# GpSimd's weight subtractions in pieces of 256 columns in a two-block transformer kernel on Trainium2

## The chip, the core and the metric

The kernel runs on one core of one Trainium2 chip. The core has TensorE (PE in the profile) for matrix products, VectorE (DVE), ScalarE (ACT) and GpSimd (POOL) for elementwise work, and SyncE (SP), whose queue issues the DMAs here. Each engine works through its own list of instructions in order and waits on semaphores for the others. The metric is the device time of one execution in microseconds; less is better.

## The reference

The reference runs two transformer blocks of two layers each on a sequence of 512 tokens of width 1024, in float32. The first block mixes a sparse attention and a stick-breaking attention; the second uses a latent attention (MLA) in its first layer and a gated linear attention (GLA) in its second. Each layer ends in an MLP with a squared ReLU:

```
hn = rms_norm(x, norm_g[0])
...                                   # projections of hn @ w_in, attentions, output products
x = x + rms_norm(mixed, norm_g[1])
hf = rms_norm(x, norm_g[2])
ff = jnp.square(jax.nn.relu(hf @ w_ff1)) @ w_ff2
return x + rms_norm(ff, norm_g[3])
```

## The kernel before

Products are made to float32 accuracy from three passes of rounded operands. Each operand x is kept as a high part h, which is x rounded to the matmul's format (written by ScalarE), and a low part l = x − h. A product is then h·h + l·h + h·l, three matmuls that add up in one PSUM bank (`mac3`, L211 to L213; for products with tokens on the partitions L238 to L240).

Weights come in units. `wload` (L169) takes a unit of, as a rule, 8 k-tiles by 256 columns or 4 k-tiles by 512, and splits it in two halves by k-tile. For each half it issues one DMA into a raw buffer (`wraw`, three buffers), has ScalarE write the high part (`wh`, L190), and has GpSimd subtract it from the raw values to give the low part (`wl`, L194). Most halves hold 1024 values per partition, so that one GpSimd instruction works on 128x1024 values. With `both`, used near the start of a stage, the half is split once more between VectorE and GpSimd, and GpSimd's share is 128x512. The pool of weights has two buffers per name, and a raw buffer is free for the next DMA when both parts have been read from it.

VectorE makes the low parts of activations (L166, `split`), adds partial sums of the MLP's second product into y (L541, one input in PSUM), squares the MLP's hidden values (L529, with both inputs in SBUF), and applies residuals and normalisation: `residual` (L301) runs L308 and L309 in turn for eight k-tiles, `newton` (L283) three short instructions on the inverse root. In the first block's second product of the conditioning vectors, spread through the MLP, VectorE also runs L1380, which has one input in SBUF and one in PSUM. In the sparse attention, `nsa_cmp` runs L996 to L1006 on the compressed scores, and TensorE transposes the result in L1010. Within the layers, GpSimd also scales softmax values (L1047, L1764) and adds some sums of squares (L299, into `acc`).

The order of each engine's instructions comes from the order in which the program emits them and a scheduler that sorts them by need; DMAs of weights, of the conditioning matrix (`araw`) and of intermediate values all go through SP's queue. Generators interleave the stages: `tick` and `fill` put steps of a normalisation or of a background product between the matmuls of a running one.

Of the kernel before, what the change touches and what calls it, by code (L numbers as in the profile page):

```python
# [11 lines left out]
F32 = mybir.dt.float32  # L12
# [3 lines left out]
ALU = mybir.AluOpType  # L16
# [34 lines left out]
class Builder:  # L51
# [117 lines left out]
    def wload(self, ap, both=False, pool=None, raws=(), after=()):  # L169

        nc = self.nc
        aps = ap if isinstance(ap, list) else [ap]
        kt, n = aps[0].shape[1], sum(a.shape[2] for a in aps)
        h = self.t(pool or self.wp, [P, kt, n], F32R, tag="wh")
        l = self.t(pool or self.wp, [P, kt, n], F32R, tag="wl")
        hk = (kt + 1) // 2
        for a, b in ((0, hk), (hk, kt)):
            if a < b:
                if raws:
                    raw = raws[a > 0]  # L180
                else:
                    raw = self.t(self.wp, [P, b - a, n], F32, tag="wraw", bufs=3)
                    c = 0
                    for x in aps:
                        nc.sync.dma_start(raw[:, :, c:c + x.shape[2]], x[:, a:b])
                        c += x.shape[2]
                step = max(1, (b - a) // 2) if both else b - a
                for x in range(a, b, step):
                    z = min(b, x + step)
                    i = nc.scalar.copy(h[:, x:z], raw[:, x - a:z - a]).ins  # L190
                    for j in after:
                        self.tc.add_manual_dep(i, j.name, NOSYNC, reason="order")
                    e = nc.vector if both and x == a else nc.gpsimd
                    e.tensor_tensor(l[:, x:z], raw[:, x - a:z - a], h[:, x:z].bitcast(F32), op=ALU.subtract)  # L194
        return h, l

    def wload_turned(self, ap, w):

        nc = self.nc
        raw = self.t(self.wp, [P, 8, 64], F32, tag="wraw", bufs=3)  # L200
        nc.sync.dma_start(raw, ap)
        x = raw.rearrange("p k (a b e) -> p k a b e", a=2, b=2)
        h, lo = (o.rearrange("p k (b a e) -> p k b a e", a=2, b=2) for o in w)
        for b in range(2):
            nc.scalar.copy(h[:, :, b], x[:, :, :, b])
            nc.gpsimd.tensor_tensor(lo[:, :, b], x[:, :, :, b], h[:, :, b].bitcast(F32), op=ALU.subtract)
# [2144 lines left out]
```

## Time and profile before

| | |
|---|---|
| median of 3 runs | 3435.24 us (3432.82 to 3436.9) |
| profiled execution | 3436.59 us, span 3434.8 us |
| TensorE busy | 3264.5 us, 95% |
| VectorE busy | 2136.6 us, 62% |
| ScalarE busy | 1511.9 us, 44% |
| GpSimd busy | 1172.7 us, 34% |
| granted clock of TensorE, mean | 0.982 |

Busy times are sums over instructions, from the start of each to its end. An instruction that has started and stands still counts as busy. Idle time of an engine that nobody waits for costs nothing. A granted clock of 1.00 in a stretch is 2.4 GHz throughout; less means that part of the stretch ran at 1.2 GHz.

### The profile page before, as it was taken

How to read it: one execution, taken by the hardware profiler on the slowest of the kernel's cores; microseconds unless marked ns; L12 is line 12 of the kernel's file. 1: busy time of each engine (PE TensorE's matmuls, PEld its weight loads, DVE VectorE, ACT ScalarE, POOL GpSimd, SP SyncE). 2: the span in 40 equal slices, each digit the busy share in tenths (PEclk: the TensorE clock that was granted, in tenths of full speed). 3: DMA queues.
4: the chain of work that ended last, by engine and by line, in shares of the span. 5: the costliest groups of instructions: out<-in, count | busy, mean ns of one | idle time of the engine just before them, and what ended most of it. 6: DMA issues, size and time to landing. Idle time of an engine off the chain costs nothing.

```text
span 3434.8 us, 48977 instructions
## 1 busy us (share of the span) xinstructions
PE 3264.5 (95%) x18723; PEld 2825.8 (82%) x18723; DVE 2136.6 (62%) x4036; ACT 1511.9 (44%) x3323; POOL 1172.7 (34%) x688
## 2 busy tenths in 40 slices
PE   8899989999889998999999999999999899989998
PEld 8788778778878877778888879888888888878887
DVE  6855676885875567676577765333344767873445
ACT  5445544232544555432256664422222566653223
POOL 3333334444323333434422222222232222124443
PEclk8999999999999999999999999999999999999999
DMA  5212464553321245465321131121222211123332
GB/s 177 65 62 71 143 195 127 189 183 110 108 68 59 71 141 178 143 201 178 93 69 33 48 98 60 62 62 62 62 62 64 67 64 55 61 78 100 98 96 70
DMA packets 262097, 337.68 MB, mean 98 GB/s; under 512 B 17107, under 2 KB 178110, under 8 KB 261734
## 3 DMA queue, kind: packets, MB, share of 16 engines
q1 hardware_dynamic: 261862, 334.55, 31.0%
q8 instruction: 147, 2.41, 0.3%
q14 instruction: 88, 0.72, 0.1%
HBM read 305.98 MB, written 28.52 MB: 97 GB/s over the span
## 4 chain that ended last, share of the span: by engine, by line
PE 68%; DVE 17%; ACT 6%; issue 5%; DMA 3%; POOL 1%; SPq 0%; DVEq 0%; ACTq 0%; POOLq 0%
PE mm L211 15%; PE mm L213 15%; PE mm L212 15%; PE s L211 4%; PE s L212 4%; PE s L213 4%; PE s L280 2%; DMA araw<-in_ada_w_dram 2%; ACT wh L190 1%; DVE tp L1380 1%; PE tp L1065 1%; POOL wl L194 1%; DVE y L308 1%; PE mm L238 1%; PE mm L239 1%
## 5 line engine op out<-in xcount | busy, mean ns | idle before, releaser
L194 POOL TENSOR_TENSOR wl<-wraw,wh 128x1024 fp32r<-128x1024 f32 (+2 forms) x424 | 990.7, 2355 | 1748.3 <-ACT wh L190 1698.6
L211 PE MATMUL mm<-h,wh 128*128 128x512 f32 (+1 forms) x1916 | 722.6, 378 | 28.2 <-ACT h L332 8.8
L212 PE MATMUL mm<-h,wl 128*128 128x512 f32 (+1 forms) x1916 | 712.0, 372 | 0.5 <-DVE wl L194 0.4
L213 PE MATMUL mm<-h,wh 128*128 128x512 f32 (+1 forms) x1916 | 709.4, 371 | 2.1 <-DVE h L333 1.8
L190 ACT CAST wh<-wraw 128x1024 fp32r<-128x1024 f32 (+3 forms) x454 | 429.0, 967 | 493.8 <-issue 290.6
L211 PEld LDWEIGHTS mm<-h,wh 128*128 128x128 f32 x1916 | 367.6, 192 | 89.4 <-ACT h L332 9.6
L213 PEld LDWEIGHTS mm<-h,wh 128*128 128x128 f32 x1916 | 367.0, 192 | 64.0 <-DVE h L333 3.1
L212 PEld LDWEIGHTS mm<-h,wl 128*128 128x128 f32 x1916 | 368.1, 192 | 52.2 <-DVE wl L194 0.8
L529 DVE TENSOR_TENSOR t<-t 128x512 f32<-128x512 f32 (+1 forms) x140 | 173.0, 1235 | 253.1 <-ACT hid L525 252.9
L211 PE MATMUL mm<-hid,wh 128*128 128x512 f32 (+1 forms) x848 | 293.8, 346 | 11.8 <-DVE y L541 9.6
L212 PE MATMUL mm<-hid,wl 128*128 128x512 f32 (+1 forms) x848 | 290.9, 343 | 0.0
L213 PE MATMUL mm<-hid,wh 128*128 128x512 f32 (+1 forms) x848 | 290.5, 343 | 0.0
L1380 DVE SCALAR_TENSOR_TENSOR tp<-araw,sc,tp 128x512 f32<-128x512 f32 x280 | 200.5, 749 | 51.1 <-DMA araw<-in_ada_w_dram 50.0
L541 DVE TENSOR_TENSOR y<-y,mm 128x512 f32<-128x512 f32 (+1 forms) x192 | 105.4, 549 | 193.7 <-PE mm L213 193.5
L530 DVE TENSOR_TENSOR hid<-t,hid 128x512 fp32r<-128x512 f32 (+1 forms) x176 | 205.6, 1172 | 31.5 <-ACT t L527 26.3
L213 PE MATMUL s<-hid,wh 128*128 128x512 f32 (+1 forms) x560 | 208.7, 373 | 0.0
L211 PE MATMUL s<-hid,wh 128*128 128x512 f32 (+1 forms) x560 | 208.6, 373 | 0.0
L212 PE MATMUL s<-hid,wl 128*128 128x512 f32 (+1 forms) x560 | 208.2, 372 | 0.0
L525 ACT ACTIVATE hid<-t 128x512 fp32r<-128x512 f32 (+1 forms) x176 | 97.1, 554 | 241.7 <-DVE t L522 165.9
L211 PEld LDWEIGHTS mm<-hid,wh 128*128 128x128 f32 x848 | 160.0, 189 | 38.2 <-DVE y L541 6.8
L212 PEld LDWEIGHTS mm<-hid,wl 128*128 128x128 f32 x848 | 160.1, 189 | 20.9
L213 PEld LDWEIGHTS mm<-hid,wh 128*128 128x128 f32 x848 | 160.0, 189 | 21.0
(686 smaller groups left out, 7337.1 us busy)
## 6 DMA issues: line engine op xcount, KB each, us to landing
wraw<-in_w_ff_dram SPq DMA_DIRECT2D x128, 512.0 KB
wraw<-in_mlp_w_dram SPq DMA_DIRECT2D x128, 512.0 KB
araw<-in_ada_w_dram SPq DMA_DIRECT2D x96, 512.0 KB
wraw<-in_w_in_dram SPq DMA_DIRECT2D x68, 512.0 KB
raw<-in_cmp_w_dram SPq DMA_DIRECT2D x16, 512.0 KB
td<-t SPq DMA_DIRECT2D x32, 256.0 KB
h<-td SPq DMA_DIRECT2D x32, 256.0 KB
wraw<-in_w_out_dram SPq DMA_DIRECT2D x16, 512.0 KB
```

The source lines that it names most:

```text
L190: i = nc.scalar.copy(h[:, x:z], raw[:, x - a:z - a]).ins
L194: e.tensor_tensor(l[:, x:z], raw[:, x - a:z - a], h[:, x:z].bitcast(F32), op=ALU.subtract)
L211: nc.tensor.matmul(ps, wh, mh, start=first, stop=False)
L212: nc.tensor.matmul(ps, wl, mh, start=False, stop=False)
L213: nc.tensor.matmul(ps, wh, ml, start=False, stop=last)
L238: nc.tensor.matmul(ps, h[:, sl], w[0][:, k, :n], start=k == 0, stop=False)
L280: self.nc.tensor.matmul(ps, self.ones, acc, start=first, stop=last)
L525: nc.scalar.activation(h, a, AF.Square)
L529: nc.vector.tensor_tensor(a, a, a, op=ALU.mult)
L530: nc.vector.tensor_tensor(lo, a, h.bitcast(F32), op=ALU.subtract)
L541: nc.vector.tensor_tensor(y, y, ps, op=ALU.add)
L1380: nc.vector.scalar_tensor_tensor(a, raw[:, k], sc, a, op0=ALU.mult, op1=ALU.add)
```

## The change

GpSimd's subtraction is written as a loop over the k-tiles of the half and, in each, over runs of at most 256 columns. VectorE's share under `both` stays one instruction.

```diff
-                    e = nc.vector if both and x == a else nc.gpsimd
-                    e.tensor_tensor(l[:, x:z], raw[:, x - a:z - a], h[:, x:z].bitcast(F32), op=ALU.subtract)
+                    if both and x == a:
+                        nc.vector.tensor_tensor(l[:, x:z], raw[:, x - a:z - a], h[:, x:z].bitcast(F32),
+                                                op=ALU.subtract)
+                    else:
+                        self.low_parts(l[:, x:z], raw[:, x - a:z - a], h[:, x:z])
         return h, l
+
+    def low_parts(self, l, raw, h):
+
+        for k in range(l.shape[1]):
+            for c in range(0, l.shape[2], 256):
+                s = slice(c, min(c + 256, l.shape[2]))
+                self.nc.gpsimd.tensor_tensor(l[:, k, s], raw[:, k, s], h[:, k, s].bitcast(F32), op=ALU.subtract)
```

The lists of TensorE, VectorE, ScalarE and SyncE keep every instruction in its place; line numbers after the change are larger by 10. GpSimd's list goes from 440 instructions of this line to 1636. In the latent attention two softmax scalings (L1764) that stood behind a whole half of a unit now stand ahead of that half's last piece; all other GpSimd instructions keep their neighbours.

GpSimd's list in the first block's second layer, where the weights of the background product (`wl`) meet the first softmax scalings (`pb`), is this before:

```order
L194 TENSOR_TENSOR wl_9557<-wraw_9558,wh_9556 128x1024
L194 TENSOR_TENSOR wl_9557<-wraw_9562,wh_9556 128x1024
L194 TENSOR_TENSOR wl_9848<-wraw_9849,wh_9847 128x1024
L194 TENSOR_TENSOR wl_9848<-wraw_9853,wh_9847 128x1024
L1047 TENSOR_SCALAR pb_9819<-pb_9819,cf_9837 128x256 x2
```

The same place after the change:

```order
L205 TENSOR_TENSOR wl_9911<-wraw_9912,wh_9910 128x256 x4
L205 TENSOR_TENSOR wl_9911<-wraw_9919,wh_9910 128x256 x4
L205 TENSOR_TENSOR wl_10208<-wraw_10209,wh_10207 128x256 x4
L205 TENSOR_TENSOR wl_10208<-wraw_10216,wh_10207 128x256 x4
L1057 TENSOR_SCALAR pb_10179<-pb_10179,cf_10197 128x256 x2
```

Each half of a unit is four instructions in place of one, at the same place in the list.

GpSimd's list in the second block's last layer, where the sums of squares (`acc`) of the output product stand between the halves of the MLP's first weights, before:

```order
L299 TENSOR_TENSOR acc_95<-acc_95,t_30203 128x256
L194 TENSOR_TENSOR wl_30457<-wraw_30458,wh_30456 128x1024
L299 TENSOR_TENSOR acc_95<-acc_95,t_30323 128x256
L194 TENSOR_TENSOR wl_30457<-wraw_30462,wh_30456 128x1024
L299 TENSOR_TENSOR acc_95<-acc_95,t_30342 128x256
```

And after:

```order
L309 TENSOR_TENSOR acc_95<-acc_95,t_31207 128x256
L205 TENSOR_TENSOR wl_31461<-wraw_31462,wh_31460 128x256 x4
L309 TENSOR_TENSOR acc_95<-acc_95,t_31327 128x256
L205 TENSOR_TENSOR wl_31461<-wraw_31469,wh_31460 128x256 x4
L309 TENSOR_TENSOR acc_95<-acc_95,t_31346 128x256
```

The sum of squares in the middle still stands between the two halves, now behind four pieces and ahead of four.

## Rows read from the trace of the kernel before

**Rows 1.** The page's busy times: engine, us, share, instructions.

```profile
PE 3264.5 (95%) x18723; PEld 2825.8 (82%) x18723; DVE 2136.6 (62%) x4036; ACT 1511.9 (44%) x3323; POOL 1172.7 (34%) x688
```

**Rows 2.** Stretches: us; busy of PE, PEld, DVE, ACT, POOL; granted clock; DMA.

```profile
510.00:850.00 340.00, 340.00 (x1544) 274.57 (x1543) 249.77 (x359) 113.49 (x168) 143.87 (x59) 1.00 0.48 151
850.00:985.00 135.00, 117.30 (x838) 107.88 (x836) 110.46 (x259) 69.40 (x180) 47.64 (x33) 0.96 0.33 96
...
2720.00:3070.00 350.00, 314.67 (x2180) 289.26 (x2179) 253.60 (x682) 211.23 (x635) 83.53 (x40) 0.95 0.21 64
```

**Rows 3.** TensorE's waits: instruction, what ended it: us in total, times, longest.

```profile
PE tp L1010 <- DVE sc L1006: 15.2, 6, 3.8
PE s L280 <- ACT y L322: 13.4, 15, 3.1
PE mm L211 <- DVE y L541: 11.4, 8, 2.2
PE mm L211 <- ACT h L332: 8.8, 4, 3.9
PE tp L968 <- DVE qhl L166: 7.8, 6, 3.2
...
PE tp L2140 <- DVE gyt L2134: 6.5, 3, 3.0
PE s L2029 <- DVE ggl L166: 5.6, 4, 1.8
PE s L1747 <- ACT mpb L146: 5.5, 3, 4.5
...
PE mm L211 <- DVE y L609: 5.1, 1, 5.1
```

**Rows 4.** Groups by form: busy us, mean ns of one, idle time before them.

```profile
L194 POOL TENSOR_TENSOR wl<-wraw,wh 128x1024 fp32r<-128x1024 f32 x368 | 907.3, 2485 | 1529.6 <-ACT wh L190 1486.6 <-issue 42.8
...
L529 DVE TENSOR_TENSOR t<-t 128x512 f32<-128x512 f32 x112 | 135.3, 1208 | 234.3 <-ACT hid L525 234.1
L541 DVE TENSOR_TENSOR y<-y,mm 128x512 f32<-128x512 f32 x96 | 65.6, 683 | 163.6 <-PE mm L213 163.5
```

**Rows 5.** Timeline 966 to 977 us: start, us, engine, instruction.

```profile
970.80 4.87 POOL L194 TENSOR_TENSOR wl<-wraw,wh 128x1024 fp32r<-128x1024 f32 x2 [18.04 <-issue]
...
970.99 2.48 DVE L1005 TENSOR_TENSOR sc<-sc,vis 128x256 f32<-128x256 f32 x1
973.39 2.30 DVE L1004 TENSOR_TENSOR cst<-cst,gates 128x8 f32<-128x8 f32 x1
...
975.95 0.41 DVE L1006 TENSOR_TENSOR sc<-sc,cst 128x256 f32<-128x256 f32 x1
...
976.41 0.62 PE L1010 MATMUL tp<-ident,sc 128*128 128x128 f32 x2 [3.83 <-DVE sc L1006]
```

**Rows 6.** Timeline 608 to 614 us, GpSimd and VectorE in an MLP.

```profile
608.22 4.79 POOL L194 TENSOR_TENSOR wl<-wraw,wh 128x1024 fp32r<-128x1024 f32 x2 [4.82 <-ACT wh L190]
...
611.52 2.06 DVE L1380 SCALAR_TENSOR_TENSOR tp<-araw,sc,tp 128x512 f32<-128x512 f32 x3
```

**Rows 7.** Timeline at 865 us: a 256-column GpSimd instruction with two inputs.

```profile
865.12 0.73 POOL L299 TENSOR_TENSOR acc<-acc,sq 128x256 f32<-128x256 f32 x1 [10.73 <-ACT sq L298]
```

**Rows 8.** The chain that ended last, 1250 to 1350 us, by line.

```profile
by line: issue 42.1%; POOL wl L194 18.3%; DMA araw<-in_ada_w_dram 14.8%; DVE tp L1380 8.0%; DVE acc L299 1.6%; DVE y L308 1.5%; DVE ry L287 1.4%; DVE tp L1378 1.4%; DVE wl L194 1.3%; DVE x L309 1.3%; DVE sal L166 1.3%; ACT sbe L146 1.2%; AC
```

**Rows 9.** Timeline 3032 to 3040 us, VectorE and GpSimd in a residual.

```profile
3032.36 0.42 DVE L309 TENSOR_TENSOR x<-x,y 128x256 f32<-128x256 f32 x1
...
3035.58 3.42 DVE L309 TENSOR_TENSOR x<-x,y 128x256 f32<-128x256 f32 x2
...
3035.34 0.90 POOL L299 TENSOR_TENSOR acc<-acc,t 128x256 f32<-128x256 f32 x1
3036.20 2.52 POOL L194 TENSOR_TENSOR wl<-wraw,wh 128x1024 fp32r<-128x1024 f32 x1
```

## The prediction, made before the changed kernel had run

> **What bounds the kernel now.** I read the page's busy times first: TensorE is busy 95% of the span [rows 1]. So at most 3434.8 − 3264.5 = 170.3 us can be won without touching a matmul, and the only question is what ends TensorE's idle time. The view of stretches says where it lies [rows 2]: in an MLP stretch such as 510 to 850 us TensorE has no idle time at all, while between the stretches it loses 135 − 117.3 = 17.7 us (850 to 985) and 350 − 314.7 = 35.3 us (2720 to 3070). GpSimd works in all of them.
>
> The view of TensorE's waits comes next [rows 3]. Nine of its rows add up to 15.2 + 13.4 + 11.4 + 8.8 + 7.8 + 6.5 + 5.6 + 5.5 + 5.1 = 79.3 us in 50 waits. All of them are ended by VectorE or ScalarE; GpSimd, whose instructions the change rewrites, ends none. So GpSimd's own speed is not what TensorE waits for. What can matter is what GpSimd does to VectorE.
>
> That is seen in the groups by form [rows 4]. Two VectorE instructions of one size, 128x512, take 1.208 us (L529, both inputs in SBUF) and 0.683 us (L541, one input in PSUM). The timeline shows why. In [rows 5] GpSimd runs two weight subtractions, 970.80 to 975.67. L1005, with both inputs in SBUF, takes 2.48 us where L1006 of the same size takes 0.41, and it ends at 973.47, halfway through the pair; L1004, smaller still, takes 2.30 and ends at 975.69, with the pair. TensorE waits 3.83 us for L1006 behind them. In [rows 6] the same GpSimd pair runs beside L1380, which has one input in PSUM: three of those take 2.06 us, 0.69 each, and nobody is held up. So a VectorE instruction with two SBUF inputs that meets a GpSimd instruction stands still until that one instruction ends.
>
> **The change, part by part.** Only GpSimd's list differs. 368 subtractions of 1024 columns [rows 4] become four each and the other 72, of 304 to 768 columns, two to four each: 440 instructions become 1636. Two softmax scalings of the latent attention (L1764) now stand ahead of one such piece that was part of an instruction ahead of them; I cost this at nothing, since neither starts later for it and neither issues a DMA.
>
> *GpSimd's own time.* A 256-column subtraction with two inputs takes 0.73 us there [rows 7]; four take 2.92, where one of 1024 takes half of an undisturbed pair, 4.79 / 2 = 2.40 [rows 6]. That is 0.52 us more each, 368 × 0.52 = 191 us on an engine that is idle for two thirds of the span. What covers it is the lead with which weights are made, since no wait in [rows 3] ends on GpSimd. If the cover is gone it costs 0.52 us per subtraction at the places where the chain of waits runs through GpSimd: in 1250 to 1350 us it does so for 18.3% of 100 us, 18.3 us [rows 8], and at 2.92 / 2.40 = 1.22 times that it is 4 us more. Bounds: 0, where the slower link is absorbed by the 42.1% of "issue" beside it, and 9 us, if each piece also lets one VectorE instruction pass and takes 0.90 us, as a 256-column one beside L309 does [rows 9]: 4 × 0.90 = 3.6 against 2.40, half as much again. The queue behind these pieces holds GpSimd's later pieces and its sums of squares (L299), which the next normalisation needs. I take 5 us.
>
> The Trainium skill (SBUF — State Buffer, "Who interferes with whom") calls the port pair of VectorE and GpSimd an exclusive lock held for a whole instruction, and says that whoever starts first makes the other wait. Read against this change, it means that GpSimd too is stopped once per piece, so four times where it was stopped once. The trace agrees as far as the 256-column instruction beside L309 goes: 0.90 us [rows 9] against 0.73 alone [rows 7]. By that rule the term is the upper bound above, 9 us in place of 5, and 4 us less are won.
>
> *What comes off VectorE.* A block now lasts at most one piece, 0.73 us, in place of up to 2.40. In [rows 5] the two blocked instructions lost 2.48 − 0.41 = 2.07 and at least 2.30 − 0.41 = 1.89, together 3.96 us, which is all of the 3.83 us that TensorE waited. With pieces, three instructions of that chain have two SBUF inputs and can each be caught once: at most 3 × 0.73 = 2.2 us, on average half of that. The wait then shrinks by 1.8 to 2.9 us, 46% to 75%.
>
> *Where nothing comes off.* [Rows 9] show the other kind of place. L309 takes 0.42 us alone; two of them take 3.42 beside GpSimd instructions of 0.90 and 2.52, so they lose 2.6. But there the VectorE instructions with two SBUF inputs stand back to back. Each would meet the next piece: five pieces let five instructions through in 5 × 0.73 to 5 × 0.90, 3.7 to 4.5 us, and before, two got through in 3.42 and three more would follow in 3 × 0.42, 4.7 us. The block is cut up, not shortened. The 5.1 us wait for L609 is of this kind.
>
> *The sum.* Bounds for the 79.3 us: nothing (all places dense) and all of it. Leaving out the 5.1 and taking 60%, inside the 46% to 75% of the example that I could work out, gives 0.6 × 74.2 = 44.5 us. The other 91 us of TensorE's idle time are short waits, the start, the end and DMA; I count none of it. What is late next at the shortened waits is the rest of the same VectorE and ScalarE chains, and this is why I don't take more than 60%.
>
> *The clock.* The stretches with idle time have a granted clock of 0.96 and 0.95, the MLP stretch 1.00 [rows 2]: part of them runs at the lower level, 1.2 GHz. The loss is at most 0.04 × 135 = 5.4 and 0.05 × 350 = 17.5 us, 23 together. If TensorE idles less before those places, part of it returns; bounds 0 and 23, and I take 10, somewhat under half, as the waits shrink by somewhat over half.
>
> Net: −44.5 − 10 + 5 = about −50 us. The profiled execution took 3436.6 us (span 3434.8), 1.4 over the median of 3435.2, so the forecast is 3436.6 − 50 = 3387, or **3386 us** beside the median.
>
> **Rivals.**
>
> *A, cut up but not shortened.* If most places are as dense as [rows 9], VectorE loses the same time in more portions. For it: the residual and normalisation code is a row of two-input instructions, and it stands at most stage ends. Against it: the waits for L1006, for the `qhl` and `ggl` parts and for `gyt` follow chains in which reductions, PSUM reads and ScalarE stand between. Time: −15 to +5, 3420 to 3441 us.
>
> *B, nearly all of it.* If the chains have slack elsewhere, all 74 us go, the clock returns most of its 23, and some of the uncounted 91 us too. For it: in [rows 5] the blocks alone exceed the wait. Against: other engines come next. Time: 3436.6 − 74 − 20 = 3343 us.
>
> *C, slower: GpSimd keeps the port.* Four queued pieces might run as one, with no opening for VectorE. Each block that lasted to the end of one instruction, 2.40 us, would then last 2.92; at 50 waits that is up to 50 × 0.52 = 26 us, with the 5 above 3436.6 + 31 = 3468 us. It decides from the point where a blocked VectorE instruction does not return before the fourth piece ends. Against it: in [rows 5] L1005 gets through between two GpSimd instructions that stand back to back.
>
> The Trainium skill (GPSIMD Engine Reference, "Instruction dispatch") says that a GpSimd core begins the next instruction as soon as it has finished its own share, with no barrier among the eight cores. That would speak for C, since the port need never be quite free; the end of L1005 in mid-pair speaks against it here.
>
> **How the numbers follow.** Forecast 0.64, A 0.20, B 0.10, C 0.06. About 0.2%, 7 us, is what a measurement of this kernel can tell from no change. Half of A's cases are faster by more than that, 0.10, 0.07 lie within, 0.03 are slower. So faster 0.64 + 0.10 + 0.10 = 0.84, within 0.07, slower 0.03 + 0.06 = 0.09. The range reaches from B's time, 3340, to the middle of A's, 3432: C and A's upper part stay outside above, a little of B below.
>
> **What would show it.** In the profile after: VectorE's L529 at 128x512 well under 1.208 us, and no single block over about 0.8 us; GpSimd's 256-column subtraction at 0.73 to 0.90 us and its busy time near 1172.7 + 191, more with the stops; the wait for L1006 under 8 us in place of 15.2; the wait for L609 about as before; a granted clock above 0.95 in the stretch from 2720 us. TensorE waits that end on GpSimd, or blocks of 2.9 us, would prove the forecast wrong; so would VectorE's busy time falling without TensorE's idle time falling, which is A.

## The result and the profile after

The kernel after took 3376.03 us (median of 4 runs, 3370.99 to 3377.15) beside 3435.58 us for the kernel before on the same chip: a ratio of 0.9828, with a 95% interval of 0.9816 to 0.984. The forecast was 3386 us, 10 us above. The span of the profiled execution fell by 59.9 us, from 3434.8 to 3374.9.

The page's busy times, engine by engine, answer to [rows 1]:

```profile
PE 3248.4 (96%) x18723; PEld 2812.0 (83%) x18723; DVE 1925.8 (57%) x4036; ACT 1513.9 (45%) x3323; POOL 1413.2 (42%) x1884
```

TensorE's idle time is 3374.9 − 3248.4 = 126.5 us where it was 170.3, so 43.8 us of the gain are idle time. The other 16.1 us are busy time, 3264.5 to 3248.4 for the same 18723 matmuls; the mean granted clock rose from 0.982 to 0.987. VectorE's busy time fell by 210.8 us for the same 4036 instructions, though not one of them was touched. GpSimd's rose by 240.5 us.

The view of stretches, between the same matmuls as in [rows 2]; behind the length stand the busy times of PE, PEld, DVE, ACT and POOL, the granted clock and the DMA share:

```profile
491.82:831.82 340.00, 340.00 (x1545) 274.56 (x1543) 228.38 (x359) 113.46 (x168) 175.06 (x233) 1.00 0.47 151
831.82:962.42 130.60, 116.05 (x839) 104.97 (x837) 104.88 (x259) 69.60 (x181) 59.67 (x73) 0.99 0.34 100
2675.89:3011.69 335.80, 309.55 (x2180) 284.68 (x2179) 240.34 (x682) 212.41 (x635) 105.16 (x134) 0.97 0.21 67
```

The MLP stretch is as long as before, 340.00 us, although VectorE got rid of 21 us of it. The two others became 4.4 and 14.2 us shorter, and their clocks went from 0.96 to 0.99 and from 0.95 to 0.97.

TensorE's waits (what it did, what ended the wait: us in all, times, longest) answer to [rows 3]; line numbers are larger by 10:

```profile
PE s L290 <- ACT y L332: 17.0, 19, 3.5
PE mm L221 <- ACT h L342: 9.6, 5, 4.2
PE tp L978 <- DVE qhl L166: 6.8, 7, 2.4
...
PE tp L1020 <- DVE sc L1016: 4.6, 6, 1.0
PE tp L2150 <- DVE gyt L2144: 4.6, 3, 2.0
...
PE mm L221 <- DVE y L551: 4.3, 2, 2.2
...
PE s L2039 <- DVE ggl L166: 1.9, 4, 0.6
...
PE mm L221 <- DVE y L619: 1.9, 1, 1.9
...
PE s L1757 <- ACT mpb L146: 1.5, 4, 0.9
PE s L904 <- POOL wl L205: 1.4, 4, 0.5
...
PE mm L222 <- POOL wl L205: 0.8, 1, 0.8
```

The waits for L1016, the old L1006, fell from 15.2 to 4.6 us, the longest of them from 3.8 to 1.0. Those for `ggl`, for `mpb` and for L551 (the old L541) fell by 3.7, 4.0 and 7.1. Two did not fall: for ScalarE's y, 13.4 before, and for its h, 8.8 before. The last two rows are new: GpSimd now ends some waits itself.

The groups by form (busy us, mean ns of one, idle time before), for [rows 4]:

```profile
L205 POOL TENSOR_TENSOR wl<-wraw,wh 128x256 fp32r<-128x256 f32 x1576 | 1208.2, 803 | 1485.6 <-ACT wh L190 1398.4 <-issue 82.5 <-DVE x L319 3.4
...
L539 DVE TENSOR_TENSOR t<-t 128x512 f32<-128x512 f32 x112 | 89.2, 796 | 275.6 <-ACT hid L535 275.4
...
L551 DVE TENSOR_TENSOR y<-y,mm 128x512 f32<-128x512 f32 x96 | 65.7, 684 | 200.0 <-PE mm L223 200.0
```

L539 (the old L529, both inputs in SBUF) takes 796 ns where it took 1208. L551, with one input in PSUM, takes 684 as before. A GpSimd piece takes 803 ns, and four of them 3.21 us where one whole instruction took 2.49.

The timeline of [rows 5] (start, us, engine, instruction, how many), from 951 to 956 us:

```profile
950.96 5.25 POOL L205 TENSOR_TENSOR wl<-wraw,wh 128x256 fp32r<-128x256 f32 x7 [15.75 <-issue]
...
951.15 0.83 DVE L1015 TENSOR_TENSOR sc<-sc,vis 128x256 f32<-128x256 f32 x1
...
951.90 0.70 DVE L1014 TENSOR_TENSOR cst<-cst,gates 128x8 f32<-128x8 f32 x1
...
952.86 0.68 DVE L1016 TENSOR_TENSOR sc<-sc,cst 128x256 f32<-128x256 f32 x1
...
953.60 0.44 PE L1020 MATMUL tp<-ident,sc 128*128 128x128 f32 x2 [0.86 <-DVE sc L1016]
```

The blocked instruction goes with the end of the piece beside it, not with the end of the half: 0.83 and 0.70 us for L1015 and L1014, where the old L1005 and L1004 took 2.48 and 2.30. L1016 now meets a piece too and takes 0.68 in place of 0.41. TensorE waits 0.86 us there, before 3.83.

### The profile page after: what moved, and what is told of

Read it like the earlier page. It is cut to its first block, busy times and chain, and to the rows that moved or that the text cites. A ratio compares the mean times of both kernels' runs of the same rounds, so it can differ in the third digit from the quotient of the medians.

```text
span 3374.9 us, 50339 instructions
## 1 busy us (share of the span) xinstructions
PE 3248.4 (96%) x18723; PEld 2812.0 (83%) x18723; DVE 1925.8 (57%) x4036; ACT 1513.9 (45%) x3323; POOL 1413.2 (42%) x1884
## 5 line engine op out<-in xcount | busy, mean ns | idle before, releaser
L205 POOL TENSOR_TENSOR wl<-wraw,wh 128x256 fp32r<-128x256 f32 x1604 | 1222.9, 799 | 1509.6 <-ACT wh L190 1422.4
L222 PEld LDWEIGHTS mm<-h,wl 128*128 128x128 f32 x1916 | 366.0, 191 | 50.1
L539 DVE TENSOR_TENSOR t<-t 128x512 f32<-128x512 f32 (+1 forms) x140 | 105.7, 755 | 292.8 <-ACT hid L535 292.6
L551 DVE TENSOR_TENSOR y<-y,mm 128x512 f32<-128x512 f32 (+1 forms) x192 | 105.6, 550 | 229.3 <-PE mm L223 229.1
L534 ACT ACTIVATE t<-mm 128x512 f32<-128x512 f32 (+1 forms) x94 | 48.1, 512 | 260.4 <-PE mm L223 260.3
```

Source lines behind the costliest of these rows:

```text
L205: self.nc.gpsimd.tensor_tensor(l[:, k, s], raw[:, k, s], h[:, k, s].bitcast(F32), op=ALU.subtract)
L222: nc.tensor.matmul(ps, wl, mh, start=False, stop=False)
L534: nc.scalar.activation(a, ps, AF.Relu)
L539: nc.vector.tensor_tensor(a, a, a, op=ALU.mult)
L551: nc.vector.tensor_tensor(y, y, ps, op=ALU.add)
```

## The experiments

The table gives the ratio to the kernel before on the same chip, and from each profile VectorE's busy time, which shows how long it stood still, and GpSimd's.

| run | us | ratio (95% interval) | VectorE | GpSimd |
|---|---|---|---|---|
| before | 3433 to 3436 | 1 | 2136.6 | 1172.7 |
| after | 3376.03 | 0.9828 (0.9816–0.984) | 1925.8 | 1413.2 |
| p512 | 3401.05 | 0.9905 (0.9892–0.9919) | 2017.6 | 1255.7 |
| p128 | 3384.46 | 0.9856 (0.9842–0.9869) | 1898.4 | 1691.4 |
| inner | 3432.69 | 0.9997 (0.9988–1.0006) | 2018.9 | 1278.2 |
| edges | 3375.91 | 0.9829 (0.9815–0.9842) | 2035.8 | 1304.8 |
| memset | 3285.18 | 0.9572 (0.9557–0.9586) | 1771.1 | 1021.9 |
| memlate | 3286.06 | 0.9575 (0.9559–0.959) | 1773.5 | 1102.2 |
| longer | 3461.37 | 1.0087 (1.007–1.0104) | 2073.5 | 1446.4 |
| late256 | 3394.64 | 0.9889 (0.9873–0.9906) | 1936.5 | 1667.4 |
| mix | 3369.27 | 0.9817 (0.9802–0.9832) | 2032.0 | 1343.0 |
| mix2 (mix once more) | 3370.61 | 0.9818 (0.9803–0.9834) | 2033.1 | 1343.4 |
| again (after once more) | 3374.35 | 0.9828 (0.9813–0.9842) | 1928.9 | 1409.6 |

The theory was that of the prediction: VectorE instructions with two SBUF inputs stand still until the GpSimd instruction beside them ends, and what counts is that this end comes sooner, at places where TensorE waits for VectorE. The rivals were that something else in the change makes the gain (weights that arrive in smaller parts), and that GpSimd's longer work decides.

In the runs of piece sizes and places (p512, p128, inner, edges, mix) TensorE, VectorE, ScalarE and the DMAs keep the order of the kernel before. In the four with fills (memset, memlate, longer, late256) the scheduler moved a few instructions: 103, 179, 63 and 63 of the 18723 places in TensorE's list and 235, 336, 118 and 99 of the 4036 in VectorE's hold another one than before.

**p512: pieces of 512 columns.**

```diff
-        for k in range(l.shape[1]):
-            for c in range(0, l.shape[2], 256):
-                s = slice(c, min(c + 256, l.shape[2]))
-                self.nc.gpsimd.tensor_tensor(l[:, k, s], raw[:, k, s], h[:, k, s].bitcast(F32), op=ALU.subtract)
+        step = max(1, 512 // l.shape[2])
+        for k in range(0, l.shape[1], step):
+            ks = slice(k, min(k + step, l.shape[1]))
+            for c in range(0, l.shape[2], 512):
+                s = slice(c, min(c + 512, l.shape[2]))
+                self.nc.gpsimd.tensor_tensor(l[:, ks, s], raw[:, ks, s], h[:, ks, s].bitcast(F32), op=ALU.subtract)
```

> Pieces of 512 values in place of 256. The theory of the block (a VectorE instruction with two SBUF inputs stands until the one GpSimd instruction it met has ended, so what counts is the length of that instruction): a whole subtraction blocked for up to 2.1 us, a 512 piece for about 1.0, a 256 piece for about 0.5. From 2.1 to 0.5 won 60 us, so from 2.1 to 1.0 should win about 40: 3392 to 3402 us, VectorE's L529 at 128x512 near 0.95 us. Rival 'any cut will do' (an opening between pieces is what counts, not their length): 3376 us as with 256. Rival 'timing of GpSimd' (the gain comes from weights that are ready at other times): GpSimd is hardly slower with 512, so 3425 to 3436 us.

It took 3401.05 us, a gain of 33 us, somewhat over half of the 60 for 256, and the squaring (the old L529) took 944 ns, both as expected. The gain follows the size of the piece.

**p128: pieces of 128 columns.**

```diff
-            for c in range(0, l.shape[2], 256):
-                s = slice(c, min(c + 256, l.shape[2]))
+            for c in range(0, l.shape[2], 128):
+                s = slice(c, min(c + 128, l.shape[2]))
```

> Pieces of 128 values. Block theory: blocks of about 0.3 us, worth 5 to 10 us more than 256, but GpSimd pays its fixed time eight times for each 1024 values (0.56 us for a 128 piece in the changed kernel, eight are 4.5 us in place of 3.2 and 2.4), so GpSimd's busy time goes to about 1900 us and TensorE's waits that end on GpSimd, 2.3 us with 256, to 5 to 20: 3370 to 3390 us in all. Rival 'the smaller the better': 3360 us or less. Rival 'GpSimd becomes the bound': over 3400 us.

It took 3384.46 us and lies above the kernel after; of the four sizes 256 is the best. VectorE's busy time fell by another 27 us, but TensorE now waits for GpSimd. Its waits in p128 that GpSimd's low parts end:

```profile
PE s L904 <- POOL wl L205: 5.7, 8, 2.3
...
PE mm L222 <- POOL wl L205: 3.8, 7, 1.2
```

Over all rows of that view GpSimd ends 12.2 us of waits, where it ended 2.2 in the kernel after. A piece of 128 takes 509 ns there, so that eight of them take 4.07 us for a half: a piece of half the columns costs 63% of the time.

Something else happens with pieces of 128 that the theory excludes. A few VectorE instructions find no opening between the pieces and stand until GpSimd's whole row of them has ended:

```profile
2710.81 6.74 POOL L205 TENSOR_TENSOR wl<-wraw,wh 128x128 fp32r<-128x128 f32 x16
...
2712.40 5.29 DVE L1925 TENSOR_SCALAR gate<-t 128x256 f32<-128x256 f32 x1 [3.18 <-ACT t L1924]
...
2719.36 0.39 PE L248 MATMUL mm<-wh,h 128*128 128x256 f32 x1 [2.20 <-ACT t L1924]
```

L1925 takes 0.29 us alone; here 13 pieces pass before it ends. ScalarE's work on `gate` follows it, and TensorE then waits 2.20 us for ScalarE where it didn't wait in the kernel after. L540, with two inputs in SBUF, stood through 11 pieces at 2148 us, 4.68 us in place of 0.42. So the loss at 128 is not only GpSimd's fixed time.

**inner and edges: the pieces in one part of the program alone.** In `inner` only the units inside an MLP are cut, in `edges` all others (there False and True below change places).

```diff
+        if not self.cut:
+            self.nc.gpsimd.tensor_tensor(l, raw, h.bitcast(F32), op=ALU.subtract)
+            return
         for k in range(l.shape[1]):
...
+            self.cut = True if c <= 5 else False
             w.append(self.wload(wv[:, 4 * c:4 * c + 4, u * 512:(u + 1) * 512]))
+            self.cut = False
...
+                self.cut = True if 1 <= c <= 6 else False
                 w.append(self.wload(v1[:, :, c * 512 + u * 256:c * 512 + (u + 1) * 256], c == 0 and self.stage < 3))
+                self.cut = False
```

> Pieces of 256 only for weights of the MLPs' inner units (first product's units 1 to 6 and second product's 0 to 5), all others whole. Block theory: the blocks there lie beside matmuls that never wait, so VectorE gets about 140 us of busy time back (L529 and L530) and the time stays at 3430 to 3438 us. Rival 'VectorE's busy time is what counts': these units hold about two thirds of what VectorE won, so about 40 of the 60 us, 3396 us.

> The complement: pieces of 256 everywhere but in those inner MLP units, which stay whole. Block theory: the whole gain, 3372 to 3380 us, though VectorE's L529 stays near 1.2 us. Rival 'VectorE's busy time': about 20 us, 3415.

Inner took 3432.69 us, no change; edges 3375.91, the whole gain. The page of inner shows what this means:

```profile
PE 3260.4 (95%) x18723; PEld 2824.5 (82%) x18723; DVE 2018.9 (59%) x4036; ACT 1512.8 (44%) x3323; POOL 1278.2 (37%) x1264
```

VectorE stands still for 117.7 us less than before, more than in edges (100.8, where the squaring still takes 1130 ns), and the time is the same. In the inner units of the MLPs TensorE doesn't wait for VectorE. The busy time of VectorE tells that the mechanism is there, and not what it is worth.

**memset: GpSimd doesn't read.** GpSimd's share of the low parts is left out: it subtracts two columns and then writes zeros to the whole half twice, 227 + 2 × 956 = 2139 ns, near the 2485 of before.

```diff
-        for k in range(l.shape[1]):
...
+        self.nc.gpsimd.tensor_tensor(l[:, 0, 0:2], raw[:, 0, 0:2], h[:, 0, 0:2].bitcast(F32), op=ALU.subtract)
+        for _ in range(2):
+            self.nc.gpsimd.memset(l.bitcast(F32), 0.0)
```

> GpSimd keeps nearly its time per weight half but reads next to nothing: a subtraction of two columns, which waits for the raw values and the high part as before, and then two fills of the whole half with zero (0.96 us each for 1024 values). GpSimd's share of the low parts of the weights is zero, so the output lacks that correction. Block theory, with the block put down to GpSimd reading SBUF: VectorE's blocks by weights go, L529 at 128x512 falls to about 0.69 us, and the time falls below that of 256-value pieces: block lengths of 1.6, 0.8 and 0.37 us on average gave 3434, 3401 and 3376 us, which leads on to about 3357 at none, so 3343 to 3365. Rival 'any GpSimd instruction of that length blocks': two fills of about 1 us block like 512-value pieces, 3385 to 3405. Rival 'timing of GpSimd': 3425 to 3440.

It took 3285.18 us: 148 us less than before, and far below what was expected. Two groups by form of this run:

```profile
L538 DVE TENSOR_TENSOR t<-t 128x512 f32<-128x512 f32 x112 | 77.4, 691 | 294.9 <-ACT hid L534 294.7
...
L204 POOL MEMSET wl<- 128x1024 f32 x736 | 698.7, 956 | 33.7
```

The squaring (L538) takes 691 ns, that is its time with nothing in the way, beside GpSimd instructions of 956 ns that only write. The stretches of this run, for the second and third of [rows 2]:

```profile
813.63:928.64 115.01, 111.46 (x839) 104.20 (x837) 87.05 (x259) 69.20 (x181) 43.42 (x80) 1.00 0.37 113
2606.72:2920.12 313.40, 300.67 (x2180) 278.45 (x2179) 213.17 (x682) 210.25 (x635) 73.17 (x108) 0.99 0.23 72
```

These two alone are 20.0 and 36.6 us shorter than before, where the pieces of 256 brought 4.4 and 14.2. The expectation extended the trend of the piece sizes: a block of half the length, half the loss. That was wrong, because each cut also makes more blocks. Worked out from all VectorE instructions of the traces (each one's duration less the shortest of its form, where that is over 60 ns), the mean block is 1291 ns in 314 instructions before, 363 ns in 529 after and 247 ns in 654 in p128; the sums are 405, 192 and 162 us. Down to 128 columns, cutting comes nowhere near zero; memset has 25 us.

**memlate: the raw buffers are held as long as before.** In memset a raw buffer is free some 2 us earlier, and the next weights could load earlier. Here a second subtraction of two columns stands behind the fills.

```diff
         for _ in range(2):
             self.nc.gpsimd.memset(l.bitcast(F32), 0.0)
+        self.nc.gpsimd.tensor_tensor(l[:, 0, 0:2], raw[:, 0, 0:2], h[:, 0, 0:2].bitcast(F32), op=ALU.subtract)
```

> As the run "memset" (GpSimd's share of the low parts is zero: left out), with a second subtraction of two columns behind the two fills, so that the raw weights' buffer is held until the half is done, some 0.25 us later than in the kernel before (2.4 us). Theory, that "memset" (3285) won its time because GpSimd no longer reads operands beside VectorE: 3283 to 3300, and L540 (the first of the MLP's pair on VectorE) within 0.70 us. Rival, that much of it came from raw buffers given back 2 us earlier, and so from weights loaded earlier: 3320 to 3350 with the same VectorE durations.

It took 3286.06 us; the earlier buffers gave nothing. Its page:

```profile
PE 3216.6 (98%) x18723; PEld 2795.3 (85%) x18723; DVE 1773.5 (54%) x4036; ACT 1510.1 (46%) x3323; POOL 1102.2 (34%) x2008
```

So what memset won goes with the reading, not with earlier buffers. Two things are not separated. The moved instructions are one. The other is that in both runs TensorE multiplies by zeros in those low parts. Of the 151.3 us by which memset's span is shorter, 101.3 are idle time of TensorE (170.3 to 69.0); the other 50.1 are busy time for the same matmuls, at a mean clock of 0.994 in place of 0.982, and whether the zeros have a part in that clock no run shows. The MLP stretch, at 1.00 and 340.0 us with and without them, can't tell.

**longer: whole subtractions that end later.**

```diff
+        if l.shape[1] * l.shape[2] == 1024:
+            n = l.shape[2] // 2
+            self.nc.gpsimd.tensor_tensor(l[:, 0, 0:2], raw[:, 0, 0:2], h[:, 0, 0:2].bitcast(F32), op=ALU.subtract)
+            self.nc.gpsimd.memset(l[:, :, 0:n].bitcast(F32), 0.0)
+        self.nc.gpsimd.tensor_tensor(l, raw, h.bitcast(F32), op=ALU.subtract)
```

> The subtraction stays whole, and ahead of each of 1024 values GpSimd runs a subtraction of two columns and a fill of half the columns (about 0.7 us more GpSimd time for each, some 250 us in all; the values are the same). This is the cost of the change alone, weights that are ready later, without its shorter blocks. The prediction's term for it was 5 us, bounds 0 and 9: 3434 to 3444 us. Rival 'timing of GpSimd' (later weights are what won): 3376 to 3420. Rival 'GpSimd is close to the bound': over 3450.

It took 3461.37 us, 28 us more than before, where 10 at most were expected. GpSimd's busy time, 1446.4 us, is near that of the kernel after (1413.2), and a half is done after 277 + 527 + 2430 = 3234 ns, as the four pieces are (3212). But in this run TensorE waits for GpSimd:

```profile
PE mm L223 <- POOL wl L206: 13.2, 13, 1.6
```

That is 14.5 us with the smaller rows, and the granted clock fell from 0.982 to 0.977. The same lateness cost the kernel after 2.2 us of such waits. The reason suggested itself in the order of TensorE's list: 516 of its instructions there wait for a GpSimd instruction before the change, and 1363 after it. A matmul waits only for the piece that it reads, the first of which is done after 0.8 us, and no longer for the whole half.

**late256: the same prelude ahead of the pieces.** The edit is the first four added lines of `longer`, ahead of the loop of the kernel after. In 144 of the 368 halves one piece runs between the two-column subtraction and the fill.

> The pieces of 256 columns as in the kernel after, but each half of 1024 values is preceded by the subtraction of two columns and the zero fill of 512 columns of the run "longer" (277 and 527 ns there), so that the whole half is ready later than in any run so far (some 3.7 us after its start, against 3.2 in "longer" and 2.4 in before), while its first k-tile is ready after some 1.5 us. Theory, that TensorE waits for the pieces of a k-tile alone and the first of them is what counts: waits of TensorE for GpSimd's low parts stay below 5 us (2.3 in after, 14.6 in "longer"), time 3376 to 3388. Rival, that what made "longer" slow is the half's later end or GpSimd's longer work as such: 10 us of such waits or more, and 3398 to 3415.

It took 3394.64 us beside 3374.35 for the kernel after on the same chip, 20 us more, and between the two expectations. Its waits for low parts:

```profile
PE mm L226 <- POOL wl L209: 7.8, 14, 1.2
...
PE s L908 <- POOL wl L209: 6.5, 8, 1.5
```

With the smaller rows GpSimd ends 16.3 us of waits, 14.3 of them with low parts. So the theory as I had put it, that the first k-tile is what counts, falls: a half's first piece is ready after some 1.6 us (225 + 527 + 798 ns), sooner than the half in the kernel before. The trace says which pieces TensorE waited for. Only 1.3 of the 14.3 us end with the first piece of a half; 5.7 end with the third or fourth in the MLPs' second products. The 6.5 of L908 end with weights of which GpSimd's share is 512 values, without a prelude of their own: they stood in GpSimd's list behind others.

A prelude of 0.75 to 0.8 us costs 20 us with the pieces and 28 without, so the lead of the weights covers that much in neither form. The kernel after ends its halves as late as `longer` does and pays 2.2 us of waits where `longer` pays 14.5. That agrees with the k-tiles being released one by one, but it is not isolated by a run.

**mix: a size for each place.** Whole in the inner units of the MLPs, 128 from the second block's first output product on (where `p128` was up to 3 us faster in its stretches), 256 elsewhere, and the one large subtraction of the gate weights (L1962) in four.

```diff
+        if not self.cut:
+            self.nc.gpsimd.tensor_tensor(l, raw, h.bitcast(F32), op=ALU.subtract)
+            return
...
+            for c in range(0, l.shape[2], self.cut):
+                s = slice(c, min(c + self.cut, l.shape[2]))
...
+        self.cut = 128 if self.stage >= 2 else 256
...
+        for b in range(4):
+            nc.gpsimd.tensor_tensor(G.w2[1][:, b], w2r[:, b], G.w2[0][:, b].bitcast(F32), op=ALU.subtract)
```

> A version put together from the runs: inner MLP units whole, pieces of 128 from the second block's first output product on (where the run with 128 was about 8 us shorter than the one with 256 between the same matmuls), pieces of 256 elsewhere, and GpSimd's one other subtraction of 1024 values (the gate weights of the GLA) in four. Block theory: 3376 less 5 to 10, 3364 to 3372 us. Rival 'those 8 us were scatter between executions': 3373 to 3379.

It took 3369.27 us, within the range expected, with an interval that overlaps that of the kernel after. It was run once more beside the kernel after on one chip:

> The kernel of the run "mix" once more, beside the kernel after on one chip. If its sizes are worth what the stages say (stage sums put it 4 to 7 us below after): 3365 to 3373, with an interval of its ratio below that of the kernel after. Rival, that the stage differences are noise of one execution: within 3 us of after.

> The kernel after itself, beside the three others on one chip: 3371 to 3380. If late256 is slower than it by more than 12 us, the first k-tile alone isn't what counts.

This time 3370.61 us (ratio 0.9818, 0.9803 to 0.9834) beside 3374.35 (0.9828, 0.9813 to 0.9842). Against the kernel before on its own chip, mix came out lower than the kernel after by 0.0011 and 0.0010, some 4 us, both times; the intervals overlap and don't tell them apart. The instruction that stood for 5.29 us in p128 stands for 5.17 and 5.31 in these two.

## Why the prediction was right, and where it was not

**What bounds the kernel: right.** TensorE waits for VectorE, and VectorE for GpSimd's reading. Memset takes the reading away and 148 us go (with the zeros and the moved instructions not separated); inner and edges show that the blocks in the MLPs' inner units don't count. Of the 59.9 us of the span, VectorE's part of TensorE's idle time is the core: summed over all gaps between matmuls by what ended them, VectorE's went from 95.4 to 53.6 us, ScalarE's from 58.7 to 54.9 and GpSimd's from 0.1 to 2.3.

**The term of the nine waits: right in total by luck, wrong in its parts.** I had −44.5 us from the nine rows and nothing from the rest. Idle time fell by 43.8. But the nine rows went from 79.3 to 52.2 us, −27.1 or 34% and not 60% of 74.2; the other −16.7 came from the 91 us of short waits which I had put at nothing. Two errors cancelled. The short waits were made of blocks as well: in memset, without the reading, what is left beside the nine rows is 46 us.

**The example: right, and a little low.** The wait for L1006 was to shrink by 46% to 75%; in the place of [rows 5] it shrank by 78%, over its six occurrences by 70%. What went wrong was to carry that percentage to the other rows. The waits for h and y are ended by ScalarE, and in memset, without any reading, these two read:

```profile
PE s L289 <- ACT y L331: 8.9, 13, 1.8
PE mm L220 <- ACT h L341: 8.3, 3, 4.2
```

The wait for ScalarE's h, 8.8 before, hardly depends on the reading (in memlate it is 6.2).

**The dense place: the mechanism was right, the row was not.** Ahead of what [rows 9] show, the trace of the kernel before has one more blocked L308 and the whole subtraction that blocks it, and behind it the awaited L609:

```profile
3032.69 2.97 DVE L308 SCALAR_TENSOR_TENSOR y<-y,mod,ry 128x256 f32<-128x256 f32 x2
...
3038.93 0.41 DVE L609 TENSOR_TENSOR y<-mm,hc 128x256 f32<-128x256 f32 x1
...
3032.88 2.50 POOL L194 TENSOR_TENSOR wl<-wraw,wh 128x1024 fp32r<-128x1024 f32 x1 [8.76 <-ACT wh L190]
```

VectorE and GpSimd in the kernel after, from 2976.5 to 2985 us, the same place:

```profile
2976.75 0.75 DVE L319 TENSOR_TENSOR x<-x,y 128x256 f32<-128x256 f32 x2
2977.42 1.34 DVE L318 SCALAR_TENSOR_TENSOR y<-y,mod,ry 128x256 f32<-128x256 f32 x2
2978.69 1.81 DVE L319 TENSOR_TENSOR x<-x,y 128x256 f32<-128x256 f32 x2
2980.43 0.41 DVE L619 TENSOR_TENSOR y<-mm,hc 128x256 f32<-128x256 f32 x1
2980.76 1.49 DVE L318 SCALAR_TENSOR_TENSOR y<-y,mod,ry 128x256 f32<-128x256 f32 x2
...
2977.60 3.49 POOL L205 TENSOR_TENSOR wl<-wraw,wh 128x256 fp32r<-128x256 f32 x4 [8.76 <-ACT wh L190]
2981.05 0.91 POOL L309 TENSOR_TENSOR acc<-acc,t 128x256 f32<-128x256 f32 x1
2981.92 3.52 POOL L205 TENSOR_TENSOR wl<-wraw,wh 128x256 fp32r<-128x256 f32 x4
```

The two engines take turns, as foretold: 3.49 / 4 = 0.87 us for a piece, 1.81 / 2 = 0.90 for an L319 that takes 0.42 alone. But I had written that the wait for L609 stays at 5.1 us, and it fell to 1.9. TensorE doesn't wait for the end of this row of instructions. It waits for L619, which stands in its middle behind three blocked ones (one L318 and two L319). Before, these sat through two whole subtractions (2.50 and 2.52 us) and one instruction of 0.90, 3038.93 − 3032.88 = 6.05 us from the first of them to L609; now they sit through three pieces, 2980.43 − 2977.60 = 2.83 us. The difference is the 3.2 us by which the wait fell. I had counted five blocked instructions against pieces and only two against whole subtractions, and so missed that each blocked instruction costs one GpSimd instruction, whatever its length, up to the awaited one. The row of [rows 3] that does behave as dense is the one for ScalarE's y, which follows each L319: 13.4 before, 17.0 now, and 8.9 in memset, as above. It had been counted among those that shrink.

**The clock: right in sign, mis-sized.** −10 us was taken from bounds of 0 and 23; it gave −16.1. In the two stretches the loss went from 5.4 to 0.01 × 130.6 = 1.3 and from 17.5 to 0.03 × 335.8 = 10.1, so they returned 11.5 of them. My upper bound left out all other stretches, and those returned the rest. TensorE had 16 periods at 1.2 GHz in this trace, 27 before; that the short waits which went are the reason is argued, not shown.

**GpSimd later: smaller than taken.** +5 us against 2.2 us of waits on GpSimd. Its own price was too low, though: 240.5 us of busy time where 191 and "more with the stops" stood, since a piece takes 803 ns in the mean. TensorE waits that end on GpSimd were among my signs of a wrong forecast; five came, and I should have given the sign a size. That the cover is thin is shown by p128, longer and late256. By the reading of the Trainium skill (SBUF — State Buffer, "Who interferes with whom") that I had weighed, an exclusive lock under which GpSimd too is stopped at every piece, the term was 9 us; 2.2 us of waits came. The trace agrees that GpSimd is stopped too, 0.87 us for a piece where 0.73 is the piece alone, but not by a whole VectorE instruction each time: 0.73 + 0.42 would be 1.15.

**The rivals.** A (cut up, not shortened) is what the waits for ScalarE's y show; it didn't decide the total. B (nearly all) was refuted for this change, and the time it gave, 3343 us, was not the floor either: without the reading it is 3285. C (GpSimd keeps the port) is refuted for pieces of 256: L1015 and L1014 come through after one piece each, and the longest block beside pieces is 0.62 us. (One of 2.20 is left, beside the whole subtraction of the gate weights, L1962, which the change doesn't touch.) For pieces of 128 it is not refuted: the 5.29 and 4.68 us in p128 are what C describes, in a few places.

## What to carry to other kernels

When an instruction takes longer than its twin of the same size, look at what runs beside it on the engine that shares its inputs' memory; its price is found only where somebody waits for the slow one, and the busy time of the stalled engine doesn't say where that is. Cutting the other engine's instructions shortens each block and raises their number, so the gain flattens (33 us at 512 columns, 60 at 256, 49 at 128 here), while the fixed cost of a piece eats the lead of its consumers, and with the shortest pieces a few VectorE instructions found no opening at all until the row of pieces had ended. For a wait behind a row of blocked instructions, count the blocks up to the awaited instruction, not those of the whole row.

## What the runs showed of the hardware

- A GpSimd instruction that only writes (the fill of 128x1024, 956 ns) doesn't hold up VectorE's two-input instructions: 691 ns for L538 beside it, where 1208 ns stood beside the subtractions. That is not so for every instruction with one input: in memset L1924 (the L1925 of p128) took 1.40 us beside fills, 0.29 alone.
- A GpSimd subtraction of float32 takes 2485 ns for 1024 columns, 1376 for 512, 803 for 256 and 509 for 128, each in its run with the stops included: from 128 to 256 it is 294 ns for 128 columns, so that some 215 ns of a piece don't depend on its size (an estimate from these two).
- With pieces of 256 the two engines take turns, instruction by instruction, when both have their next one ready: 0.87 us for a piece (0.73 alone) and 0.90 for a VectorE instruction that takes 0.42 alone. With pieces of 128 this failed in a few places: a VectorE instruction stood through 11 and 13 pieces (4.68 and 5.29 us).
